# Start bytes of the SBUF tiles: three 32-byte shifts in an encoder layer

## The chip, the cores and the metric

One NeuronCore of a Trainium2 chip runs the kernel: TensorE (PE, whose weight loads the profile lists apart as PEld), VectorE (DVE), ScalarE (ACT), GpSimd (POOL) and SyncE (SP), which issues every DMA here. Data lies in SBUF, a memory of 128 partitions: a tile takes the same byte range in each of them, and "start byte" below is where that range begins, modulo 128. Matmul results lie in PSUM. The metric is the device time of one execution in microseconds, the median of several runs.

## The reference

One layer of an encoder with 1024 channels, run for a prompt of 256 tokens and a sample of 1024 tokens with shared weights (1280 tokens, ten blocks of 128). All data are float32.

```python
def trunk(x, ...):
    x = x + 0.5 * rms_norm(swiglu(rms_norm(x, ffn1_pre_g), ffn1_w_gu, ffn1_w_down), ffn1_post_g)
    x = x + rms_norm(mixer(rms_norm(x, mix_pre_g), w_in, conv_w, ..., w_out), mix_post_g)
    x = x + 0.5 * rms_norm(swiglu(rms_norm(x, ffn2_pre_g), ffn2_w_gu, ffn2_w_down), ffn2_post_g)
    return rms_norm(x, final_g)

def swiglu(h, w_gu, w_down):            # w_gu 1024 x 5632, w_down 2816 x 1024
    gate, up = jnp.split(h @ w_gu, 2, axis=-1)
    return (jax.nn.silu(gate) * up) @ w_down

def mixer(h, ...):
    q, k, v, ga, gb = split(h @ w_in)   # 8 heads of 64, 512 conv channels
    attn = dilated_attention(q, k, v)   # three (window, dilation) branches, merged by softmax weights
    c = silu(layer_norm(depthwise_conv31(ga * sigmoid(gb)) + conv_b))
    return concatenate([attn, c]) @ w_out
```

## The kernel before

Every large product is done three times in float32r: an operand is split into a high part (ACT copies it with rounding) and a low part (DVE subtracts), and `mm3` (lines 196 to 200) issues high x high, high x low (or low x high) and the other mixed product. A TensorE matmul streams the moving operand (`rh` in `mm3`) against a stationary one of 128 x 128 (`lh`) that a weight load brings in just ahead. In the profile's names, as `psd<-wd,ahl`, the first input is the moving one and the second the stationary one.

The order of the work on each engine is that of the code, which interleaves it by hand; the tile framework puts the semaphore waits in. The stages, in order: the first feed-forward block (`ffn`, matmuls into `psgu` with the token tiles `hT` moving and `whi`/`wlo` stationary; into `psd` with `whi`/`wlo` moving and `ah`/`al` stationary), the input projection with the convolution beside it (`w_in`; DVE adds 24 taps per channel group into PSUM, line 744, each reading the tile `glu` from 4 bytes further on), the attention (`attn`; q stationary, `kH` and `kL` moving, lines 952 and 953), `w_out`, and the second feed-forward block: `ffn_gu` first runs two column groups as in the first block, and then `pair`, which forms 7 products out of 8 from token sums (`T2` to `T4`, or `hT` itself) with `wb` as the weights, into `psAB`, `psC` and `psR`; then `ffn_down`, into `psd` with `wd` moving and `ahl` stationary. Ten RMS norms per norm stage go through `rstd` and the stages of `chain`, where `st` is a tile of two numbers per partition.

Where a tile begins follows from the order in which pools are opened. Pools on the left side stack upwards from the start of SBUF: `const` (the 128 x 128 identity `ident`, two scalars, `cv`), `hp` (the `hT` tiles, which later also hold the second block's results, named `yh0h` and so on), `stp` (the small statistics tiles `ast`, `bn`, `st`), `tp` (working tiles `tmp`, `x`, `g`), and then those of the stages: `fy` (`y`), `qk0`, `wc` (`cacc`), `wo1`, `fa2`/`ft2` (`ac`, `T2` to `T4`), `p2` (`wd`, `xr`). Pools with `side="right"` stack downwards from the end: `wp` and later `wp2` (`raw`, `whi`, `wlo`, `wb`, `ahl`, `ar`), `fa` (`ah`, `al`, `sg`), `wg` (`glu`), `att`, `attr` (`pr`, `pT`), `qk1`. Each tile is rounded up to a multiple of 32 bytes. Nearly all big tiles have sizes that are multiples of 128 bytes, so one start byte passes from pool to pool along each side. `run` opens the pools.

Of the kernel before, what the change touches and what calls it, by code (L numbers as in the profile page):

```python
# [10 lines left out]
F32 = mybir.dt.float32  # L11
# [6 lines left out]
P = 128  # L18
# [48 lines left out]
class Stream:  # L67
    def __init__(self, t, units, raw=None, ahead=2):
        self.t, self.units, self.rawp, self.ahead = t, units, raw, ahead
        self.raw, self.w, self.nl, self.nc = {}, {}, 0, 0  # L70
# [78 lines left out]
class Trunk:  # L149
    def __init__(self, tc, ctx, a):  # L150
        self.tc, self.nc, self.ctx, self.a = tc, tc.nc, ctx, a
        nc = self.nc
        self.const = ctx.enter_context(tc.tile_pool(name="const", bufs=1))
        self.ident = self.const.tile([P, P], F32, name="ident")
        make_identity(nc, self.ident)
        self.mhalf = self.const.tile([P, 1], F32, name="mhalf")
        nc.gpsimd.memset(self.mhalf, -0.5)
        self.zero = self.const.tile([P, 1], F32, name="zero")
        nc.gpsimd.memset(self.zero, 0.0)
        self.hp = ctx.enter_context(tc.tile_pool(name="hp", bufs=1))  # L160
        self.stp = ctx.enter_context(tc.tile_pool(name="stp", bufs=4))
        self.tp = ctx.enter_context(tc.tile_pool(name="tp", bufs=2))
        self.psg = ctx.enter_context(tc.tile_pool(name="psg", bufs=4, space=PSUM))
        self.psd = ctx.enter_context(tc.tile_pool(name="psd", bufs=2, space=PSUM))
        self.dp = ctx.enter_context(tc.tile_pool(name="dp", bufs=1, space=DRAM))
        self.hT = {}
        self.stages, self.live, self.ready, self.stale = (), [], [], set()
        self.bg = []
        self.mmn = 0
# [32 lines left out]

    def rstd(self, src, junk, mul):
        nc = self.nc
        st = self.stp.tile([P, 2], F32, name="st", tag="st", bufs=9)
        nc.scalar.activation(junk, src, AF.Square, scale=D ** -0.5 / mul, accum_out=st[:, 0:1])  # L206
        nc.gpsimd.tensor_scalar(st[:, 0:1], st[:, 0:1], 1e-6 / (mul * mul), None, op0=OP.add)  # L207
        nc.gpsimd.tensor_tensor(st[:, 1:2], st[:, 0:1], self.mhalf, op=OP.pow)
        return st[:, 1:2]
# [972 lines left out]
def run(self):  # L1182
# [9 lines left out]
    def pool_(name, **kw):  # L1192
        m = tc.tile_pool(name=name, reuse_waits="tile", **{"bufs": 1, **kw})
        p = m.__enter__()
        return p, lambda: m.__exit__(None, None, None)

    wp, wp_x = pool_("wp", bufs=10, side="right")
    self.wp = wp
    units = self.ffn_units(a["ffn1_w_gu"], a["ffn1_w_down"])
# [139 lines left out]
    self.finish()  # L1339
    p_x()  # L1340
    wp_x()


Trunk.run = run
# [25 lines left out]
```

## Time and profile before

| what | value |
|---|---|
| median of 3 runs | 2439.67 us (2438.82 to 2442.0) |
| profiled execution | 2438.86 us, its span 2437.1 us |
| mean granted TensorE clock | 0.982 |
| busy: PE, PEld, DVE, ACT, POOL | 2350.7, 2009.4, 1263.2, 739.9, 491.5 us |
| moved from and to HBM | 149.23 MB read, 43.73 MB written |

The span is from the first to the last instruction; the profiled execution's own time is 1.8 us longer. Busy time of PE counts the time from a matmul's start to its modelled end, and the matmuls overlap: a 512-wide one is listed with 389 ns, though in a row they start every 0.23 us. So the time that a row of matmuls costs is read from the starts in the timeline, not from the mean length. A row of the grouped views ends with busy time, the mean length of one instruction in ns, and the idle time of the engine before it with what ended it. The view of one line or tile gives lengths as minimum, median and maximum in ns.

### The profile page before, as it was taken

The page shows a single profiled execution, that of the slowest core. Times are in us where ns is not written, and L with a number is a line of the kernel's source. Part 1 is how long each engine was busy: PE and PEld are TensorE (multiplying, and loading weights), DVE is VectorE, ACT ScalarE, POOL GpSimd, SP SyncE. Part 2 cuts the span into 40 slices and gives each one's busy share as a digit, 9 for nine tenths or more (in the row PEclk, how much of TensorE's full clock was granted, in tenths as well). Part 3 has the DMA queues.
Part 4 walks back from the last instruction along what each step waited for, and adds up shares of the span by engine and source line. Part 5 has one row for each costly group of instructions (what it writes and reads, how often), then busy time and mean ns, then how long its engine had stood idle before and what let it go on. Part 6 is the DMA issues. An engine that isn't in the chain of part 4 may idle for free.

```text
span 2437.1 us, 30173 instructions
## 1 busy us (share of the span) xinstructions
PE 2350.7 (96%) x12028; PEld 2009.4 (82%) x12028; DVE 1263.2 (52%) x1695; ACT 739.9 (30%) x1387; POOL 491.5 (20%) x474
## 2 busy tenths in 40 slices
PE   7999999999999998999997799999999999999996
PEld 7888888888888887888886678888888888788885
DVE  5344444444444438899455553564344444454557
ACT  5211111111111125565356552332322222312113
POOL 2000000000000016797202233223232323100004
PEclk9999999999999999999998899999999999999998
DMA  5111111111111115241267552211222222432324
GB/s 179 44 35 44 35 44 35 44 35 44 35 44 35 44 61 164 70 124 61 78 157 148 112 157 95 93 57 61 72 70 68 74 62 84 130 106 68 106 74 154
DMA packets 191827, 194.92 MB, mean 80 GB/s; under 512 B 30212, under 2 KB 154916, under 8 KB 191686
## 3 DMA queue, kind: packets, MB, share of 16 engines
q1 hardware_dynamic: 191686, 193.00, 26.8%
q8 instruction: 94, 1.54, 0.3%
q14 instruction: 47, 0.39, 0.1%
HBM read 149.23 MB, written 43.73 MB: 79 GB/s over the span
## 4 chain that ended last, share of the span: by engine, by line
PE 87%; DMA 5%; DVE 3%; ACT 2%; issue 1%; POOL 1%; SPq 1%; POOLq 0%; ACTq 0%; DVEq 0%
PE psgu L198 9%; PE psgu L199 9%; PE psgu L200 9%; PE psd L198 7%; PE psd L199 7%; PE psd L200 7%; PE psAB L198 4%; PE psAB L199 4%; PE psAB L200 4%; PE psR L199 2%; PE psR L200 2%; PE psR L198 2%; PE psC L198 2%; PE psC L199 2%; PE psC L200 1%; PE psqk L198 1%
## 5 line engine op out<-in xcount | busy, mean ns | idle before, releaser
L390 DVE TENSOR_TENSOR y<-y,psd 128x1024 f32<-128x1024 f32 x190 | 231.6, 1219 | 176.2 <-PE psd L200 176.2
L207 POOL TENSOR_SCALAR st<-st 128x1 f32<-128x1 f32 x70 | 41.7, 596 | 1253.4 <-ACT tmp L206 981.8
L371 DVE TENSOR_TENSOR sg<-sg,psgu 128x512 f32<-128x512 f32 (+1 forms) x66 | 39.5, 599 | 273.0 <-PE psgu L200 273.0
L198 PE MATMUL psd<-wd,ahl 128*128 128x512 f32 x440 | 172.1, 391 | 3.3 <-DVE yh0l L663 1.4
L199 PE MATMUL psd<-wd,ahl 128*128 128x512 f32 x440 | 171.3, 389 | 0.0
L200 PE MATMUL psd<-wd,ahl 128*128 128x512 f32 x440 | 171.2, 389 | 0.0
L198 PE MATMUL psd<-whi,ah 128*128 128x512 f32 x432 | 169.7, 393 | 0.8 <-DVE y L407 0.8
L199 PE MATMUL psd<-wlo,ah 128*128 128x512 f32 x432 | 169.3, 392 | 0.0
L200 PE MATMUL psd<-whi,al 128*128 128x512 f32 x432 | 167.7, 389 | 0.0
L90 ACT ACTIVATE whi<-raw 128x1024 fp32r<-128x1024 f32 x98 | 103.2, 1058 | 212.1 <-PE psgu L199 166.9
L198 PE MATMUL psgu<-hT0h,whi 128*128 128x512 f32 (+1 forms) x416 | 155.9, 375 | 0.0
L198 PE MATMUL psgu<-hT1h,whi 128*128 128x512 f32 (+1 forms) x416 | 155.3, 373 | 0.5 <-ACT hT1h L225 0.5
L199 PE MATMUL psgu<-hT0l,whi 128*128 128x512 f32 (+1 forms) x416 | 155.6, 374 | 0.0
L200 PE MATMUL psgu<-hT0h,wlo 128*128 128x512 f32 (+1 forms) x416 | 155.4, 374 | 0.0
L91 DVE TENSOR_TENSOR wlo<-raw,whi 128x1024 fp32r<-128x1024 f32 x98 | 126.6, 1296 | 55.0 <-ACT whi L90 51.6
L199 PE MATMUL psgu<-hT1l,whi 128*128 128x512 f32 (+1 forms) x416 | 155.0, 373 | 0.0
L200 PE MATMUL psgu<-hT1h,wlo 128*128 128x512 f32 (+1 forms) x416 | 155.0, 373 | 0.0
L115 DVE TENSOR_TENSOR wb<-raw,wb 128x512 fp32r<-128x512 f32 x120 | 84.8, 708 | 106.4 <-ACT wb L114 103.9
L114 ACT ACTIVATE wb<-raw 128x512 fp32r<-128x512 f32 x120 | 75.5, 629 | 167.4 <-PE psC L200 68.0
L744 DVE SCALAR_TENSOR_TENSOR acc<-glu,cv,acc 128x1024 f32<-128x1024 f32 x96 | 121.5, 1284 | 1.8
L372 ACT ACTIVATE ah<-sg 128x512 fp32r<-128x512 f32 (+1 forms) x65 | 35.9, 553 | 253.0 <-DVE sg L371 253.0
L198 PE MATMUL psgu<-hT2h,whi 128*128 128x256 f32 x384 | 109.5, 286 | 2.8 <-DVE hT1l L226 2.8
(356 smaller groups left out, 6124.5 us busy)
## 6 DMA issues: line engine op xcount, KB each, us to landing
raw<-in_ffn_w_gu_dram SPq DMA_DIRECT2D x88, 512.0 KB
raw<-in_ffn_w_down_dram SPq DMA_DIRECT2D x22, 512.0 KB
ad<-ac SPq DMA_DIRECT2D x44, 256.0 KB
g<-in_ffn_w_down_dram SPq DMA_DIRECT2D x22, 512.0 KB
ar<-ad SPq DMA_DIRECT2D x44, 256.0 KB
raw<-in_w_in_dram SPq DMA_DIRECT2D x20, 512.0 KB
x2d<-y SPq DMA_DIRECT2D x10, 512.0 KB
q<-qd SPq DMA_DIRECT2D x16, 320.0 KB
```

The costliest lines, as they stand in the source:

```text
L90: nc.scalar.activation(hi, raw, AF.Copy)
L91: nc.vector.tensor_tensor(lo, raw, hi.bitcast(F32), op=OP.subtract)
L114: nc.scalar.activation(out[:, 0], src, AF.Copy)
L115: nc.vector.tensor_tensor(out[:, 1], src, out[:, 0].bitcast(F32), op=OP.subtract)
L198: mm(out, lh[0], rh[0], start=first, stop=False, skip_group_check=more)
L199: mm(out, lh[0], rh[1], start=False, stop=False, skip_group_check=more)
L200: mm(out, lh[1], rh[0], start=False, stop=last, skip_group_check=more)
L207: nc.gpsimd.tensor_scalar(st[:, 0:1], st[:, 0:1], 1e-6 / (mul * mul), None, op0=OP.add)
L371: nc.vector.tensor_tensor(s[:, :n], s[:, :n], ps[1][:, :n], op=OP.mult)
L372: nc.scalar.activation(ah, s[:, :n], AF.Copy)
L390: nc.vector.tensor_tensor(yb, yb, o, op=OP.add)
L744: nc.vector.scalar_tensor_tensor(V["acc"], gs(k), w(k), V["acc"], op0=OP.mult, op1=OP.add)
```

## The change

Two unused tiles of 8 numbers per partition (32 bytes) are added and the ring of `st` grows from 9 to 10 entries of 32 bytes. Nothing reads or writes the new tiles.

```diff
@@ Trunk.__init__
         nc.gpsimd.memset(self.zero, 0.0)
+        self.pad = self.const.tile([P, 8], F32, name="pad")
         self.hp = ctx.enter_context(tc.tile_pool(name="hp", bufs=1))
@@ rstd
-        st = self.stp.tile([P, 2], F32, name="st", tag="st", bufs=9)
+        st = self.stp.tile([P, 2], F32, name="st", tag="st", bufs=10)
@@ run
+    rp, rp_x = pool_("rp", side="right")
+    rpad = rp.tile([P, 8], F32, name="rpad")
     wp, wp_x = pool_("wp", bufs=10, side="right")
 ...
     wp_x()
+    rp_x()
```

The `pad` shifts everything on the left from `hp` on by 32 bytes, the longer `st` ring what follows `stp` by 32 more, and `rpad` everything on the right by 32 bytes downwards. In the built program the tiles begin here, modulo 128:

| tiles | before | after |
|---|---|---|
| `hT` (and `yh0h`, `yh0l`, `yh2h` in them) | 96 | 0 |
| left side behind the statistics: `tmp`, `x`, `g`, `y`, `cacc`, `T2` to `T4`, `ac`, `wd`, `xr`, the even heads' `q`, `qb`, `kH`, `kL` | 96 | 32 |
| right side: `raw`, `whi`, `wlo`, `wb`, `ah`, `al`, `ahl`, `ar`, `glu`, `sg`, `pr`, `pT`, `v`, the odd heads' `q`, `qb`, `kH`, `kL` | 96 | 64 |
| `ident` | 0 | 0 |
| `ast` (ring of three) | 0, 64, 32 | 64, 0, 96 |

The instructions of each engine, and their order, are the same before and after. Of the waits two differ: of the `rstd` squares on ACT, one in the first norm no longer waits for DVE and one in the last norm no longer for POOL, since the ring of `st` comes round one entry later. The 11,088 float32r matmuls of the built program (7,920 that are 512 wide, 3,168 that are 256 wide) had both operands begin at 96, but for 160 in the attention whose moving operand begins at 32 (the 16 leading elements of `kH` and `kL` are skipped). After the change the moving operand begins at 0 in 6,800 of them, with the stationary one at 64; in 1,980 at 32 against 64 (`T2` to `T4` and `wd`); in 1,420 both begin at 64; the other 888 (mostly `w_out`, the `v` projection and the attention) have other pairs of 0, 32, 64 and 96.

## The prediction

> **What bounds the kernel now.** I read the page first, its busy times and the chain that ended last.
>
> ```profile
> span 2437.1 us, 30173 instructions
> PE 2350.7 (96%) x12028; PEld 2009.4 (82%) x12028; DVE 1263.2 (52%) x1695; ACT 739.9 (30%) x1387; POOL 491.5 (20%) x474
> ...
> PE 87%; DMA 5%; DVE 3%; ACT 2%; issue 1%; POOL 1%; SPq 1%; POOLq 0%; ACTq 0%; DVEq 0%
> ```
>
> TensorE is on the chain for 87% of the span. DMA has 5% (122 us), and DVE, ACT and POOL together 6% (146 us). Next the stages, from the view of stretches (busy us and number of instructions of each engine, granted clock, DMA share, GB/s).
>
> ```profile
> 60.00:940.00 880.00, 875.38 (x4343) 744.65 (x4343) 403.47 (x404) 152.16 (x225) 24.63 (x26) 1.00 0.15 45
> 940.00:1244.00 304.00, 297.93 (x1538) 254.52 (x1539) 231.37 (x225) 152.88 (x271) 183.16 (x200) 0.99 0.30 94
> 1244.00:1440.00 196.00, 161.35 (x949) 142.08 (x949) 113.51 (x454) 125.48 (x384) 43.69 (x26) 0.89 0.69 149
> ...
> 1760.00:2130.00 370.00, 367.00 (x1925) 314.80 (x1924) 155.93 (x224) 107.49 (x180) 97.41 (x67) 1.00 0.26 81
> 2130.00:2437.00 307.00, 287.38 (x1265) 236.80 (x1263) 174.55 (x177) 70.61 (x115) 28.18 (x40) 0.97 0.32 103
> ```
>
> In the feed-forward stages PE is busy for nearly all of the stretch at a granted clock of 1.00; only the attention (1244 to 1440) and the very ends leave it idle. So the question is whether the distance from one matmul to the next changes. The timeline gives it, from the first and last start of two steady rows: 512 columns wide (`wd` moving) and 256 wide (`hT2`).
>
> ```profile
> 2199.89 0.39 PE L198 MATMUL psd<-wd,ahl 128*128 128x512 f32 x1
> ...
> 2213.49 0.39 PE L198 MATMUL psd<-wd,ahl 128*128 128x512 f32 x1
> ```
>
> ```profile
> 300.55 0.28 PE L198 MATMUL psgu<-hT2h,whi 128*128 128x256 f32 x1
> ...
> 302.47 0.28 PE L199 MATMUL psgu<-hT2l,whi 128*128 128x256 f32 x1
> ```
>
> Between the first pair lie 60 steps, 13.60 / 60 = 226.7 ns each; between the second 16, 1.92 / 16 = 120.0 ns. The 256 further columns cost 106.7 ns, so 512 columns are 213.3 ns of streaming and each matmul carries 13.3 ns that don't depend on its width. That is the only sum in this kernel large enough to matter that a start byte might set: over the 11,088 float32r matmuls it is 148 us.
>
> **The added tiles and the longer ring.** `pad` and `rpad` have no instruction, and the list of instructions on each engine is the same, so nothing is added or moved: 0 us. The two waits that fall away are on ACT squares for the tenth block, whose `st` entry was read nine norms earlier; those readers have long run, so 0 us, and what keeps covering them is the wait for the square's own input, which stays.
>
> **TensorE.** The start bytes are what changes, and the term is 11,088 times some change of the 226.7 or 120.0 ns. Its lower bound is all of the 13.3 ns gone, 148 us less. Its upper bound comes from the nearest row in which a matmul starts later than that while the engine is fed: behind 256-wide ones.
>
> ```profile
> 1865.20 0.40 PE L198 MATMUL psC<-hT1h,wb 128*128 128x512 f32 x1
> 1865.43 0.40 PE L199 MATMUL psC<-hT1l,wb 128*128 128x512 f32 x1
> 1865.67 0.39 PE L200 MATMUL psC<-hT1h,wb 128*128 128x512 f32 x1
> ```
>
> 0.24 us after the second one is 13 ns over the steady 226.7, so 148 us more. Between ends so far apart I go by rows that already differ in start byte. The attention has float32r matmuls whose moving operand begins at 32 instead of 96, still with the stationary one at 96, and others (`qb`) whose moving operand isn't one run but eight pieces of 128 bytes, each beginning at 96:
>
> ```profile
> 1293.15 0.28 PE L953 MATMUL pss<-kL,q 128*128 128x256 f32 x1
> 1293.27 0.28 PE L952 MATMUL pss<-kH,q 128*128 128x256 f32 x1
> 1293.39 0.28 PE L953 MATMUL pss<-kL,q 128*128 128x256 f32 x1
> 1293.51 0.38 PE L1060 MATMUL oa<-pT,v 128*128 128x256 f32 x1
> ```
>
> ```profile
> 1305.53 0.28 PE L953 MATMUL pss<-kL,qb 128*128 128x256 f32 x1
> 1305.65 0.28 PE L952 MATMUL pss<-kH,qb 128*128 128x256 f32 x1
> 1305.76 0.28 PE L953 MATMUL pss<-kL,qb 128*128 128x256 f32 x1
> 1305.88 0.59 PE L1060 MATMUL ob<-pT,v 128*128 128x256 f32 x2
> ```
>
> Three steps take 0.36 us at 32 (120 ns each, as at 96) and 0.35 us (117 ns) with eight unaligned pieces. If a read that crosses some 64- or 128-byte line cost part of the 13.3 ns, eight pieces would cost it eight times, and they cost nothing. The stationary side has a row too: the statistics `ast` are loaded as weights from 0, 64 and 32 in turn.
>
> ```profile
> L980 PEld LDWEIGHTS psm<-ident,ast x8: 98/98/153, 1264.9 to 1427.1; 128*36 128x36 f32 x8
> ```
>
> Minimum and median of the eight loads are both 98 ns, and a single one is longer, though the three places take turns. That none of these rows has a float32r operand at 0 or 64 is what stays open. The third question is whether engines that read the same byte range disturb each other, since all stood at 96. Over the 60 steps above they would have had to:
>
> ```profile
> 2199.89:2213.49 13.60, 13.60 (x62) 11.26 (x60) 7.85 (x9) 4.62 (x7) 0.00 (x0) 1.00 0.14 40
> ```
>
> DVE was busy for 7.85 and ACT for 4.62 of these 13.60 us, and every start still came after 0.22 or 0.23 us.  I take 0 of the 148, by the nearness of the attention's rows; both ends stay for the range.
>
> [...]
>
> **DVE, ACT, POOL.** The convolution's taps read `glu` from a place 4 bytes further on each time, so they show every start byte:
>
> ```profile
> L744 DVE SCALAR_TENSOR_TENSOR acc<-glu,cv,acc x96: 1272/1288/1296, 993.3 to 1158.1; 128x1024 f32<-128x1024 f32 x96
> ```
>
> From 1272 to 1296 ns is 1.9%, for 24 different places. If all the 146 us on the chain moved by that, it would be 2.8 us either way; I take 0, as the places 4 bytes apart show no slope.
>
> **DMA.** Every transfer into or out of a big tile begins at another byte. No row shows one transfer from two start bytes; the nearest is the same load by two heads, each its largest piece on the chain:
>
> ```profile
> 1255.28 8.68 DMA kL<-kd
> 1267.97 9.37 DMA kL<-kd
> ```
>
> They differ by 8%, which on 122 us is 10 us either way. I take 0: those two landed at the same start byte (32), so the 8% is something else, and most transfers stay at a byte that is no multiple of 128 (32 or 64 instead of 96). Only the stores of the results, from `yh0h` to `yh2h`, now begin at 0, and nine of ten lie under other work; the last is issued at 2433.52 and has 3.6 us to the span's end.
>
> ```profile
> 2433.52 0.33 SPq L271 DMA_DIRECT2D out_dram<-yh2h  x1
> ```
>
> [...]
>
> **Sum.** Profiled execution 2438.86 (span 2437.1 and 1.8 around it), plus 0 for TensorE, 0 for the vector engines, 0 for DMA. That execution is 0.8 us under the median of the runs, 2439.67; I put the new median between, at 2439.4.
>
> **Rivals.** *The fixed 13.3 ns goes where the moving operand now begins at 0.* For it: that sum is constant over all widths, as a cost of starting a read would be, and no float32r row began at 0. Against it: the eight pieces at 117 ns. It would take 6,800 x 13.3 = 90 us, giving 2349. [...] Chance 5%.
>
> *A smaller gain outside TensorE*, in the transfers of the attention and in the ends of the stages, up to the 10 us of the DMA bound: 2430 to 2434. For it: DMA is 69% busy from 1244 to 1440, where PE waits. Against: only results begin at a rounder byte than 32. Chance 11%.
>
> *Slower: operands at different bytes collide.* Before, moving and stationary operand began at the same byte, and their reads may have run in step; now 1,980 matmuls read 32 against 64 (`T2` to `T4`, `wd`). If one of the two reads were held for 13 ns, that is 1,980 x 13.3 = 26 us, 2466; it decides, at 4.9 us, from 2.5 ns each. Against it: 32 against 96 in the attention costs 120 ns as well. Chance 7%. *Slower by DMA*, the other half of that bound: 2445 to 2450, chance 7%.
>
> *The change doesn't shift the tiles*, or only some: the time would be the same, and the forecast too.
>
> **How the numbers follow.** About 0.2%, 4.9 us, is what a measurement of this kernel can tell from no change; it is 0.44 ns per float32r matmul, so even one nanosecond on each (11.1 us) would be seen. No change has 70%: 2439.4, its own range 2435 to 2444. Faster has 5 + 11 = 16%, slower 7 + 7 = 14%. The range takes in most of the two small rivals, 2430 to 2448; outside are the 12% of the two TensorE cases and a few of the DMA ones.
>
> **What would show it.** Right: in the profile after, the 60 steps of `wd` take 13.60 us and 16 steps of `hT2` take 1.92; PE's busy time is 2351 within 3; the taps lie in 1272 to 1296 ns; the five stretches keep their shares. Wrong by TensorE: a steady distance other than 226.7 or 120.0 ns, in the rows with `hT` moving for the first rival, in `wd` and `T2` to `T4` alone for the slower one. Wrong by DMA: same distances, but the attention's stretch longer or shorter than 196 us.

## The result, and the profile after

The changed kernel takes 2461.01 us (2459.36 to 2461.08), the kernel before 2439.67: a ratio of 1.0083, interval 1.006 to 1.0106. It is slower by 21.3 us. The forecast was 2439.4, in a range of 2430 to 2448.

From the page of the changed kernel, the span, busy times and chain:

```profile
span 2459.2 us, 30173 instructions
PE 2374.7 (97%) x12028; PEld 2004.3 (82%) x12028; DVE 1262.8 (51%) x1695; ACT 740.2 (30%) x1387; POOL 492.4 (20%) x474
...
PE 87%; DMA 4%; DVE 3%; ACT 2%; POOL 2%; issue 1%; SPq 0%; POOLq 0%; ACTq 0%; DVEq 0%
```

DVE, ACT and POOL are busy for the same times within 1 us; PE alone grew, by 24.0 us, and the span by 22.1 (the weight loads, PEld, are busy for 5.1 us less); the mean granted clock was 0.983, before 0.982. Now the steady rows that the prediction measured, from the timeline after: 60 steps of `wd`, and 16 steps of `hT2`.

```profile
2214.69 0.40 PE L199 MATMUL psd<-wd,ahl 128*128 128x512 f32 x1
2214.92 0.39 PE L200 MATMUL psd<-wd,ahl 128*128 128x512 f32 x1
2215.15 0.39 PE L201 MATMUL psd<-wd,ahl 128*128 128x512 f32 x1
2215.39 0.40 PE L199 MATMUL psd<-wd,ahl 128*128 128x512 f32 x1
...
2228.69 0.40 PE L199 MATMUL psd<-wd,ahl 128*128 128x512 f32 x1
```

```profile
302.57 0.28 PE L199 MATMUL psgu<-hT2h,whi 128*128 128x256 f32 x1
...
304.46 0.28 PE L200 MATMUL psgu<-hT2l,whi 128*128 128x256 f32 x1
```

The 60 steps take 14.00 us instead of 13.60, 233.3 ns each instead of 226.7. The 16 steps take 1.89 instead of 1.92, 118 ns instead of 120. The wide matmuls became slower, and the narrow ones faster. A third kind of row, with `hT1` moving and 512 columns, first and last of 48, before and then after:

```profile
80.08 0.39 PE L198 MATMUL psgu<-hT1h,whi 128*128 128x512 f32 x1
...
90.74 0.39 PE L200 MATMUL psgu<-hT1h,wlo 128*128 128x512 f32 x1
```

```profile
80.56 0.40 PE L199 MATMUL psgu<-hT1h,whi 128*128 128x512 f32 x1
...
91.33 0.39 PE L201 MATMUL psgu<-hT1h,wlo 128*128 128x512 f32 x1
```

10.66 / 47 = 226.8 ns before, 10.77 / 47 = 229.1 after. The loss is spread over the whole program, as four places in the timelines show, each the start of the same matmul before and after:

```profile
55.26 0.40 PE L198 MATMUL psgu<-hT2h,whi 128*128 128x256 f32 x2
...
874.00 0.28 PE L198 MATMUL psgu<-hT2h,whi 128*128 128x256 f32 x1
...
1609.17 0.28 PE L198 MATMUL psgu<-hT2h,whi 128*128 128x256 f32 x1
...
2104.69 0.28 PE L199 MATMUL psR<-hT2l,wb 128*128 128x256 f32 x1
```

```profile
55.59 0.40 PE L199 MATMUL psgu<-hT2h,whi 128*128 128x256 f32 x2
...
881.27 0.28 PE L199 MATMUL psgu<-hT2h,whi 128*128 128x256 f32 x1
...
1623.55 0.28 PE L199 MATMUL psgu<-hT2h,whi 128*128 128x256 f32 x1
...
2119.93 0.28 PE L200 MATMUL psR<-hT2l,wb 128*128 128x256 f32 x1
```

Taking differences, the first 55 us lose 0.3 us, the first feed-forward block 6.9, the middle of the layer 7.1, the product pairs 0.9 and the rest, up to the span's end, 6.9: together 22.1. For the kinds of matmul I took, from the single starts in the trace, the mean time from a matmul's start to the next one's, wherever that comes within 300 ns; the last column is its change times their number in the trace of before (`T*` is `T2` to `T4`, "projections" the matmuls of `w_in`):

| rows | before, ns | after, ns | worth, us |
|---|---|---|---|
| `psd<-wd,ahl` | 226.8 | 233.3 | +8.4 |
| `psAB<-T*,wb` | 226.7 | 233.5 | +4.9 |
| `hT` moving, 512 columns (`psgu`, `psC`, `psAB`, projections) | 226.7 to 229.0 | 229.3 to 230.1 | +8.3 |
| `hT` stationary, 512 columns (`pso`, `psv`) | 226.4 to 227.9 | 233.0 to 233.9 | +4.1 |
| `psd<-whi,ah` and its two others | 227.1 to 228.6 | 229.2 to 231.8 | +2.8 |
| `hT2` moving, 256 columns, `psR` | 119.4 | 114.8 | -4.4 |
| `hT2` moving and other 256 columns, `psgu` | 121.5 to 122.3 | 120.1 to 120.8 | -2.2 |
| 256 columns, projections | 119.9 to 121.4 | 117.5 to 128.0 | +0.8 |

With 0.8 for what is left this makes +23.5, of a span longer by 22.1. What remained to be found is what in the start bytes sets this spacing.

### The profile page after: what moved, and what is told of

It is laid out like the page before. It is cut to its first block, busy times and chain, and to the rows that moved or that the text cites. A ratio compares the mean times of both kernels' runs of the same rounds, so it can differ in the third digit from the quotient of the medians.

```text
span 2459.2 us, 30173 instructions
## 1 busy us (share of the span) xinstructions
PE 2374.7 (97%) x12028; PEld 2004.3 (82%) x12028; DVE 1262.8 (51%) x1695; ACT 740.2 (30%) x1387; POOL 492.4 (20%) x474
## 4 chain that ended last, share of the span: by engine, by line
PE 87%; DMA 4%; DVE 3%; ACT 2%; POOL 2%; issue 1%; SPq 0%; POOLq 0%; ACTq 0%; DVEq 0%
PE psgu L199 9%; PE psgu L201 9%; PE psgu L200 9%; PE psd L199 8%; PE psd L201 7%; PE psd L200 7%; PE psAB L200 4%; PE psAB L201 4%; PE psAB L199 4%; PE psqk L199 2%; PE psC L201 2%; PE psC L200 2%; PE psR L201 1%; PE psR L200 1%; PE psR L199 1%; PE psqk L201 1%
## 5 line engine op out<-in xcount | busy, mean ns | idle before, releaser
L199 PE MATMUL psd<-wd,ahl 128*128 128x512 f32 x440 | 175.4, 399 | 2.5 <-DVE yh0l L664 1.4
L200 PE MATMUL psd<-wd,ahl 128*128 128x512 f32 x440 | 173.3, 394 | 0.0
L201 PE MATMUL psd<-wd,ahl 128*128 128x512 f32 x440 | 173.2, 394 | 0.0
L91 DVE TENSOR_TENSOR wlo<-raw,whi 128x1024 fp32r<-128x1024 f32 x98 | 126.2, 1291 | 57.5 <-ACT whi L90 54.0
L745 DVE SCALAR_TENSOR_TENSOR acc<-glu,cv,acc 128x1024 f32<-128x1024 f32 x96 | 121.5, 1284 | 1.8
L371 ACT ACTIVATE sg<-psgu 128x512 f32<-128x512 f32 (+1 forms) x66 | 34.4, 521 | 259.6 <-PE psgu L201 259.6
```

Source lines behind the costliest of these rows:

```text
L91: nc.vector.tensor_tensor(lo, raw, hi.bitcast(F32), op=OP.subtract)
L199: mm(out, lh[0], rh[0], start=first, stop=False, skip_group_check=more)
L200: mm(out, lh[0], rh[1], start=False, stop=False, skip_group_check=more)
L201: mm(out, lh[1], rh[0], start=False, stop=last, skip_group_check=more)
L745: nc.vector.scalar_tensor_tensor(V["acc"], gs(k), w(k), V["acc"], op0=OP.mult, op1=OP.add)
```

## The experiments

Two names for what follows: the spacing is the time from one matmul's start to the next one's in a steady row, and the distance is the start byte of the moving operand minus that of the stationary one, modulo 256 bytes. Counted modulo 256, all the big tiles of the kernel before begin at 224, so nearly every distance there is 0. After the change `hT` begins at 0, the left side at 32 and the right side at 192, so the distance is 64 for the 6,720 matmuls with `hT` moving (the 6,800 ahead of the prediction have 80 of the attention in them), 96 for 1,980 with `wd` or `T2` to `T4`, 192 where `hT` is stationary (32 in half of `pso`, whose weights stand on the left side), and still 0 for the 1,296 of `psd<-whi,ah` and its two others.

**Matmul rows alone, 16 pairs of start bytes.** A kernel that leaves the layer out (its outputs are zeros) and has nothing but rows of 192 matmuls, three per step as in `mm3`, on resident tiles. Moving and stationary operand begin at 0, 32, 64 or 96, named `a` to `d`; first 512 columns (`w`), then 256 (`n`).

```diff
+    for n, w in ((512, "w"), (256, "n")):
+        for m in range(4):
+            for s in range(4):
+                o = rows(nc, ps, M, W, f"{w}mv{LET[m]}st{LET[s]}", 32 * m, 32 * s, n)
```

> A kernel of matmul rows alone: for each of 16 pairs of start bytes (moving 0, 32, 64, 96 by stationary 0, 32, 64, 96, letters a to d in the PSUM tile's name: mv, then st), 192 float32r matmuls in the kernel's pattern of three, 512 wide, and then the same 256 wide. The outputs are zeros. Theory 1 (the pair): the distance between matmuls depends on moving minus stationary byte, so the four equal pairs give 226.7 and 120.0 ns as the kernel did with 96 and 96, and unequal pairs give 229 to 237 ns (512) and 113 to 118 ns (256). Theory 2 (each operand by itself): one row or one column of the table is slow, whatever the other operand, and 0/0, 32/32, 64/64 differ from 96/96. Theory 3 (not the last 7 bits of the address): no pair differs from another by more than 2 ns, and the slow rows of the changed kernel come from something else.

Two of the 32 rows, each by one of its three kinds of matmul (the view of a tile: length as minimum, median, maximum, then the first and last start): both at 64, and 0 against 64.

```profile
L34 PE MATMUL wmvcstc<-mvh,stl x64: 389/389/397, 462.8 to 505.7; 128*128 128x512 f32 x64
```

```profile
L34 PE MATMUL wmvastc<-mvh,stl x64: 393/394/398, 106.6 to 150.7; 128*128 128x512 f32 x64
```

63 steps of three take 42.9 us in the first, 227 ns per matmul, and 44.1 in the second, 233.3. From the single starts (the mean without the first 24 steps): all four equal pairs have 226.7 ns with 512 columns and 120.0 with 256; of the unequal ones the two whose moving operand begins 64 bytes past the stationary one 228.9, the ten others 233.3 to 234.3. With 256 columns every unequal pair took 116.7 to 118.4 but one (120.0). What else worked meanwhile, in the view of stretches:

```profile
100.00:700.00 600.00, 600.00 (x2593) 486.51 (x2592) 9.69 (x14) 0.00 (x0) 0.00 (x0) 1.00 0.00 1
```

Beside 14 copies on DVE (9.69 of 600 us) no other engine was at work, and DMA moved 1 GB/s. TensorE's own two operands suffice. The start byte of one by itself does nothing among these four, since the equal pairs are alike: the theory of the pair holds, and the two others fall.

**Everything at one byte modulo 128.** If equality modulo 128 were the rule, a placement with all tiles at 0 should be as quick as all at 96.

```diff
+        self.pad = self.const.tile([P, 8], F32, name="pad")
 ...
+    rp, rp_x = pool_("rp", side="right")
+    rpad = rp.tile([P, 24], F32, name="rpad")
```

> The kernel before with everything at 0 modulo 128 (hT, left side and right side), by padding alone. Theory 1: operands begin at the same byte again, so the distances are 226.7 and 120.0 ns and the time is 2438 to 2442 us. Theory 2: it depends on what 0 is worth by itself; since the changed kernel has hT at 0 and its 512-wide rows at 229.6 ns, some 2455 to 2465 us. Theory 3: 2440 or 2460, with no link to the bytes.

2473.9 us in a single run, against 2439.27 of the kernel before beside it: the slowest of all, and outside what each theory had given. The rows with `hT` or `wd` moving and 512 columns took 232 to 233 ns. So modulo 128 was the wrong measure: here the left side stands at 0 and the right side at 128 modulo 256.

**Rows alone, twelve distances.** The same kind of kernel, 144 matmuls per row.

```diff
+DIST = {0: "zero", 4: "four", 8: "eight", 16: "sixteen", 32: "x", 64: "xx", 96: "xxx", 128: "xxxx", 160: "xxxxx",
+        192: "xxxxxx", 224: "xxxxxxx", 256: "full"}
 ...
+    for n, w in ((512, "w"), (256, "n")):
+        for d in DIST:
+            o = rows(nc, ps, M, W, f"{w}{DIST[d]}", d, n, 128)
 ...
+    for cols, w in ((64, "half"), (32, "quarter")):
+        for d in (0, 32, 96):
+            o = rows(nc, ps, M, W, f"{w}{DIST[d]}", d, 512, cols)
```

> Matmul rows alone (the outputs are zeros), stationary operand at a fixed place, moving operand 0, 4, 8, 16, 32, 64, 96, 128, 160, 192, 224 and 256 bytes further on (modulo 512; the names zero, four, eight, sixteen, x to xxxxxxx for 32 to 224, full for 256), 144 matmuls each, 512 and then 256 wide; at the end stationary operands of 64 and 32 columns (half, quarter), 512 wide, at 0, 32 and 96. Theory 1b (the distance modulo 256): 0 and 256 give 226.7 and 120.0 ns, 128 gives about 233 (512 wide) as the kernel with all tiles at 0 had; 160, 192 and 224 repeat what -96, -64 and -32 gave: 234, 233 and 233 (512), 117, 118 and 118 (256). If the weight load's read is what the stream collides with, the narrow stationary operands lose less: 32 columns at distance 32 or 96 lie no more than 2 ns over their own distance 0. Theory 2b (the distance modulo 128, and something else made the kernel with all at 0 slow): 128 gives 226.7 and 120.0. Theory 4 (the load has no part in it): 64 and 32 columns lose 6 to 7 ns at 32 and 96 as 128 columns do.

Rows with 128 (`wxxxx`) and 256 bytes (`wfull`), and with 256 columns at 0 (`nzero`) and 192 (`nxxxxxx`):

```profile
L34 PE MATMUL wxxxx<-mvh,sth x48: 392/394/398, 251.4 to 284.3; 128*128 128x512 f32 x48
```

```profile
L34 PE MATMUL wfull<-mvh,sth x48: 389/389/395, 385.9 to 417.9; 128*128 128x512 f32 x48
```

```profile
L34 PE MATMUL nzero<-mvh,sth x48: 278/283/283, 418.6 to 435.5; 128*128 128x256 f32 x48
```

```profile
L34 PE MATMUL nxxxxxx<-mvh,sth x48: 276/276/286, 571.7 to 587.7; 128*128 128x256 f32 x48
```

47 steps take 32.9 us at 128 and 32.0 at 256 (233 and 227 ns), with 256 columns 16.9 at 0 and 16.0 at 192 (120 and 113 ns). So 256 bytes are as good as 0, and 160, 192 and 224 give what -96, -64 and -32 gave in the pairs (234.3, 233.3 and 233.3 ns with 512 columns): the period is 256 bytes. Most distances stand in the table further down. With fewer stationary columns the load is shorter; the 64-column row at distance 0, its weight load and its matmul:

```profile
L34 PEld LDWEIGHTS halfzero<-mvh,sth x48: 134/134/138, 622.3 to 654.6; 128*64 128x64 f32 x48
L34 PE MATMUL halfzero<-mvh,sth x48: 388/394/397, 622.4 to 654.8; 128*64 128x512 f32 x48
```

The load takes 134 ns instead of 188, yet the spacing is 230.0 ns at 0, 230.9 at 32 and 230.0 at 96; with 32 columns it is 231.7, 233.4 and 233.4. The narrow rows lose less to the distance, as expected if the load has a part in it, but at distance 0 they are slower than the full one (226.7), which no theory had said.

**The whole kernel at distance 0, at another byte.** All tiles at 0 modulo 256 instead of 224.

```diff
+        self.pad = self.const.tile([P, 8], F32, name="pad")
 ...
+    rp, rp_x = pool_("rp", side="right")
+    rpad = rp.tile([P, 56], F32, name="rpad")
```

> The kernel before with all big tiles at 0 modulo 256 (before: 224; in the kernel with all at 0 modulo 128 the left side was at 0 and the right side at 128 modulo 256). Theory 1b: all distances are 0 modulo 256 again, 226.7 and 120.0 ns and 2438 to 2442 us. Theory 2b or an effect of the place 0 itself: 2460 to 2475 us.

2436.81 us against 2439.55: the loss of the change is gone, though every start byte is another than in the kernel before. From the kernel with everything at one byte modulo 128 it differs only in `rpad`, which is 128 bytes longer, and these are worth 37 us.

**One part of the change alone.** First the left side at distance 96 (`wd`, `T2` to `T4`, and the half of `pso` with weights there) and `hT` at 0; then `hT` at distance 64 and the left side at 0.

```diff
 left side alone
-        st = self.stp.tile([P, 2], F32, name="st", tag="st", bufs=9)
+        st = self.stp.tile([P, 2], F32, name="st", tag="st", bufs=12)
 hT alone
+        self.pad = self.const.tile([P, 16], F32, name="pad")
-        st = self.stp.tile([P, 2], F32, name="st", tag="st", bufs=9)
+        st = self.stp.tile([P, 2], F32, name="st", tag="st", bufs=15)
```

> One part of the change alone: the left side behind the statistics 96 bytes on, so that T2 to T4 and wd stand 96 past wb and ahl (modulo 256) as in the changed kernel, while hT and the right side stay. Theory 1b: wd and T rows take 233.3 ns in the pattern 231, 232, 237, 2,040 x 6.6 = 13 us, so 2451 to 2455 us; the rows with hT moving stay at 226.7 and 120.0. Rival (the change's cost lies in hT or in other engines): 2438 to 2442 us.

> The other part alone: hT 64 bytes past the right side's tiles (modulo 256) as in the changed kernel, the left side's other tiles equal to the right side's. Theory 1b, by the first table: 3,840 512-wide matmuls x 2.2 = +8 us, 2,880 256-wide ones x -2.2 = -6 us, 720 with hT stationary x 6.7 = +5 us, and some 4 us where rows of equal distance follow unequal ones and need some 8 matmuls to settle: 2448 to 2454 us. Rival (T and wd alone carry the cost): 2438 to 2442 us.

Measured 2455.74 and 2456.14 us, against 2439.55. Sixty steps of `wd` in the timeline, the first kernel and then the second:

```profile
2196.75 0.40 PE L198 MATMUL psd<-wd,ahl 128*128 128x512 f32 x1
...
2210.75 0.40 PE L198 MATMUL psd<-wd,ahl 128*128 128x512 f32 x1
```

```profile
2202.92 0.39 PE L199 MATMUL psd<-wd,ahl 128*128 128x512 f32 x1
...
2216.52 0.39 PE L199 MATMUL psd<-wd,ahl 128*128 128x512 f32 x1
```

14.00 and 13.60 us: the `wd` rows are slow only where the left side was moved. The rows with `hT` behave the other way round: `psgu` with 512 columns at 226.7 ns in the first and 229.5 in the second, and `psv`, which has `hT` stationary, at its old 226 to 227 in the first and 233 to 234 in the second. Both times, of one run each, are above what was expected (2451 to 2455, 2448 to 2454), the first by less than 1 us, while 15 runs of the kernel before spread over 8. The two parts, 16.2 and 16.6 us, sum to 11.4 more than the 21.3 of the change.

By the groups (the kinds of matmul in the table above), the guess for the first left out `pso`, which loses 1.7 us, and rows that kept their distance, which lose some 2. In the second the 256-column rows save 2.3 us and not the 6 expected. Rows at distance 0 lose too when their neighbours are at another one: with `hT` moved, `psd<-whi,ah` and its two others 3.0 us (2.8 in the change) and `T2` to `T4` 1.5.

That the parts don't add up has no single cause. By the groups they lose 9.8 us more than the change: `psR` 2.5 (at the same distance 64 it took 117.8 ns with `hT` alone moved and 114.8 in the change), `T2` to `T4` 2.0, the rows with `hT` stationary 1.8 (half of `pso` loses in both parts), `hT` moving with 512 columns 1.7 and the other 256-column rows of `psgu` 1.7. What a row takes depended a little on the rows beside it, as these 3.0 ns of `psR`.

**Only the distance, not the byte modulo 128.** The kernel before with the right side 128 bytes further down, so every tile stays at 96 modulo 128.

```diff
+    rp, rp_x = pool_("rp", side="right")
+    rpad = rp.tile([P, 32], F32, name="rpad")
```

> The kernel before with only the right side moved by 128 bytes: every tile still begins at 96 modulo 128, but 9,204 matmuls now have their two operands 128 bytes apart modulo 256 (some 6,400 of them of 512 columns). Main theory (the distance modulo 256): 512 columns at 232 to 234 ns and 256 columns at 118 to 119, some 6,400 x 6.5 = 41 us more and 2,800 x 1.3 = 4 us less, 2470 to 2480 us; psd<-whi,ah, whose operands stay at 0, near its 228 ns. Rival (the start byte modulo 128 is what counts): 2437 to 2442 us and no spacing moved.

2472.32 us, against 2440.98 (2437.64 to 2444.97) of the kernel before. The first and last of the 48 `hT1` matmuls that took 10.66 us before:

```profile
80.65 0.40 PE L198 MATMUL psgu<-hT1h,whi 128*128 128x512 f32 x1
...
91.61 0.39 PE L200 MATMUL psgu<-hT1h,wlo 128*128 128x512 f32 x1
```

10.96 us, 233.2 ns each; `psR` went from 119.4 to 118.7, and `psd<-whi,ah` and its others, still at 0, from 228 to 230. One unused tile of 128 bytes costs 31 us, in a single run, and the byte modulo 128 cannot be the cause.

**Rows alone again, in another order.** Distances 0, 16, ... 240.

```diff
+DIST = {16 * i: f"d{chr(97 + i)}" for i in range(16)}
```

> Matmul rows alone (the kernel's computation is left out, outputs are zeros): moving operand 0, 16, 32 ... 240 bytes past the stationary one modulo 256, 512 and 256 columns, 144 matmuls each. Main theory (only the distance modulo 256 sets the spacing): the values that the earlier rows gave come back to 0.1 ns: 512 columns 226.7 at 0, 231.7 at 16, 233.3 at 32, 228.9 at 64, 233.4 at 96; 256 columns 120.0 at 0, 113.3 at 16, 116.6 at 32, 117.8 at 64, 120.0 at 96, 113.3 at 192. For the new distances: 512 columns between 226.7 and 238, none under 226.7; 256 columns between 113.3 and 123. Rival (the row that stood ahead sets the state in which the next row runs): the same distance gives other values here, since other rows stand ahead of it, by more than 1 ns in several of them.

Means from the single starts, ns, of the two runs of rows alone:

| distance | 0 | 16 | 32 | 64 | 96 | 128 | 160 | 192 | 224 | 256 |
|---|---|---|---|---|---|---|---|---|---|---|
| 512 columns, first order | 226.7 | 231.7 | 233.3 | 228.9 | 233.4 | 233.4 | 234.3 | 233.3 | 233.3 | 226.7 |
| 512, second order | 226.7 | 231.7 | 233.4 | 228.9 | 233.3 | 232.4 | 234.3 | 233.4 | 233.3 | |
| 256 columns, first order | 120.0 | 113.3 | 116.6 | 117.8 | 120.0 | 118.7 | 117.4 | 113.3 | 118.3 | 120.0 |
| 256, second order | 120.0 | 118.7 | 116.7 | 117.8 | 120.0 | 118.7 | 117.3 | 113.3 | 118.3 | |

With 512 columns the distance fixes the spacing, to 0.1 ns but for 128. No distance was under 226.7; the worst was 4, at 237.9. The other steps of 16 gave 231 to 235, and 240 gave 226.7 again. With 256 columns most come back too, but 16 gave 113.3 once and 118.7 once: there the rival, that the row ahead chooses between states, has a point. The pairs of the first experiment had 117.8 at 192, where both orders here gave 113.3.

**A version to beat both.** Since 0 is the best for 512 columns and among the worst for 256, `hT2`, whose rows as moving operand all have 256 columns, gets a distance of its own: 192 on top of the placement at 0 modulo 256, with the tiles behind it padded back to 0.

```diff
+        if t == 2:
+            self.hp.tile([P, 48], F32, name="hpad", tag="hpad")
         self.hT[t] = ...
-        st = self.stp.tile([P, 2], F32, name="st", tag="st", bufs=9)
+        st = self.stp.tile([P, 2], F32, name="st", tag="st", bufs=11)
```

> The kernel with every pair of operands at distance 0 modulo 256 except hT2, which begins 192 bytes past the right side's weights, where the rows alone took 113.3 ns instead of 120.0 with 256 columns. Main theory: 2,496 matmuls with hT2 as moving operand, up to 6.7 ns each, 16.6 us, less 0.6 us for the 144 of 512 columns that read hT2 as stationary operand, and less what the first matmuls of each row take to settle: 2421 to 2428 us, psR spacing 113 to 115 ns, wd steps unchanged at 226.7. Rival 1 (the short rows never settle in the kernel): 2433 to 2438 us. Rival 2 (TensorE is no longer the only bound once it is faster, so waits take the gain): the spacing falls, but the time stays within 3 us of 2436.8.

> All operands at 0 modulo 256, so the distances between them modulo 256 are those of the kernel before, which has all at 224. Main theory: the spacings are the same and so is the time, 2436 to 2440 us, ratio 0.998 to 1.000; what is left of the 2.7 us in the single look comes from no matmul row. Rival (the start byte itself counts a little, beside the distance): 2434 to 2437.5 us with an interval wholly below 1, and spacings of 512 columns lower by 0.5 to 1 ns.

Against 2441.04 us of the kernel before (2436.65 to 2444.62 in 15 runs): 2430.56 with `hT2` at 192, ratio 0.996 (0.9947 to 0.9972); 2437.44 without, ratio 0.9987 (0.9978 to 0.9996). The first is faster than the kernels before and after the change. The first and last of the 16 `hT2` steps:

```profile
299.29 0.28 PE L201 MATMUL psgu<-hT2h,whi 128*128 128x256 f32 x1
...
301.17 0.28 PE L202 MATMUL psgu<-hT2l,whi 128*128 128x256 f32 x1
```

1.88 us, 117.5 ns, and 117.8 in `psR`, not the 113.3 of the rows alone: it is the spacing that the pairs of the first experiment had at 192, the other of the two states. So the time is 2430.6, between the 2421 to 2428 expected and the rival's 2433 to 2438. From the groups, the 256-column rows give back 4.8 us and the 512-column ones beside them 1.6 (`hT` moving 1.2, `psd<-whi,ah` and its others 0.6, `pso` and `psv` lose 0.2); the profiled span is 7.3 us shorter than before. For the placement at 0 alone the interval lies just below 1, as both theories allow, but no row is faster: each group of float32r matmuls is worth the same within 0.2 us. What makes those 3.6 us, if they are real, stays open, and they are a third of the 10.5 above.

**`hT2` 32 bytes off.** The kernel before with `hT2` alone at distance 32, where both orders had agreed on 116.7.

```diff
+        if t == 2:
+            self.hp.tile([P, 8], F32, name="hpad", tag="hpad")
-        st = self.stp.tile([P, 2], F32, name="st", tag="st", bufs=9)
+        st = self.stp.tile([P, 2], F32, name="st", tag="st", bufs=16)
```

> The kernel before with hT2 alone 32 bytes past the right side's weights, all else at distance 0. The rows alone gave 116.7 ns at 32 in both orders in which they were run, against 120.0 at 0, and 113.3 at 192, where the kernel had 117.5. Main theory as it now stands (a distance other than 0 has several states and the rows ahead choose between them): spacing of the 256-column rows 115 to 119 ns, 2,496 x 1 to 5 ns, 2428 to 2437 us. Rival (the distance alone sets it): 116.7 ns to 0.3, and 2430 to 2433 us.

2438.44 us, ratio 0.9986 (0.9976 to 0.9996), `psR` at 116.9 and long `psgu` rows at 116.7: the spacing that the distance alone gives, but less time saved than either theory said (2428 to 2437, 2430 to 2433). The 256-column groups save 3.6 us; the 512-column ones give 1.2 back, 0.7 of it in `pso` and `psv`, which read `hT2` as stationary operand, now at 224. The comparison of times has 2.5.

## Why the prediction was wrong

**The failed step is "I take 0 of the 148, by the nearness of the attention's rows".** It put the cost of unequal start bytes for 512-column rows at nothing, from rows of 256 columns. Those rows did differ in distance (64 and 192 by the count modulo 256), but with 256 columns these distances cost nothing: 117.8 ns at 64 and 113 to 118 at 192 against 120.0 at 0, in the rows alone. With 512 columns the same distances cost 2.2 and 6.6 ns, and 96 costs 6.6, which no row of before could show, since there all 512-column rows stood at 0.

The two attention rows were also read too finely. "120 ns each" and "117 ns" are 0.36 and 0.35 us over three steps, from starts rounded to 0.01 us. By the single starts in the trace of before both take 353 ns, 117.7 each. So the row "as at 96" was already 2.3 ns faster than a row at distance 0, and "32 against 96 in the attention costs 120 ns as well" was not so: a sign that the distance mattered lay under the rounding. (The eight pieces of a `qb` row begin at distances 0 and 128 in turn.) The 98 ns of the `ast` loads compare lengths of loads, and the length of a load did not move with the change in the 512-column rows (187 or 188 ns in the median of each kind, before and after); what moved is the spacing of the matmuls.

**The 13.3 ns.** They were taken as one cost that doesn't depend on width, since 256 further columns cost 106.7 ns. At distance 192 they cost 120.0 (233.3 less 113.3), so what a distance adds is not a fixed sum per matmul. The first bound, all of it gone, was never near at 512 columns: 226.7 is the least of all rows; with 256 the distance took half of them at best (113.3 for 120.0, in the rows alone). The upper bound of 13 ns more was twice the 6.6 that came; it too was read from rounded starts, which are 235 ns apart in the trace, 8 ns over.

**The rivals.** "Operands at different bytes collide" was right that a pair at unequal bytes costs time, and had 7%; that it is a collision stays open. It named 1,980 matmuls at 13.3 ns, 26 us. They cost 6.7 ns each, 13.3 us by the groups; 9.4 us more came from rows that it left out (`hT` moving and stationary, and their neighbours, +15.2) and from the 256-column ones that gained (-5.8). So its 2466 was near by luck, two errors that cancel. Its condition, 2.5 ns each, was met. The argument against it, 120 ns in the attention, is the failed step again. "The fixed 13.3 ns goes where the moving operand begins at 0" fell: with 512 columns those rows are slower, by 2.3 ns in the steady row shown, and of those with 256 `psR` is faster by 4.6, far from 13.3. The rivals outside TensorE fell, as the next point shows. That the tiles don't shift fell with the rows.

**Other engines, DMA, added tiles.** These zeros held. The taps took 1267 to 1291 ns, where 1272 to 1296 was forecast, and the attention's `pss` matmuls lie between the same two starts as before, 166.5 us and then 165.9, in the view of the tile before and after:

```profile
L953 PE MATMUL pss<-kL,q x80: 277/282/420, 1244.9 to 1411.4; 128*128 128x256 f32 x80
```

```profile
L954 PE MATMUL pss<-kL,q x80: 275/282/420, 1256.5 to 1422.4; 128*128 128x256 f32 x80
```

The DMA bound of 10 us was not needed. That engines reading beside TensorE don't disturb it holds too: the rows alone show the spacings of the kernel's steady rows (226.7 ns at 0, 233.3 at 96).

**The forecast's own test** worked: "a steady distance other than 226.7 or 120.0 ns ... in `wd` and `T2` to `T4` alone for the slower one" is what the trace shows, except for "alone".

**What stays open.** The cause of the loss, the distance, is shown; how it acts is not. That the next weight load and the running matmul collide is supposed; no run shows it. For it speak that the distance of the two operands decides, with a period of 256 bytes, that it was worth up to 11 ns of 227 in the rows alone (237.9 ns at 4 bytes), where hardly anything else was at work (in the first of these runs DVE for 9.69 of 600 us), and that in the row shown from that run, both operands at 64, each load starts at most 0.01 us behind a matmul's start and lasts 187 or 188 ns of the 227. Against it speaks that shorter loads don't help: with 64 and 32 stationary columns the rows take 230.0 and 231.7 ns at distance 0, more than with 128. A row without weight loads was not tried. Nor is it known what chooses the state of a 256-column row.

## What to carry to other kernels

Where TensorE bounds a float32r kernel, as here (87% of the chain), print the start bytes of both matmul operands modulo 256 and their difference: unused tiles of 32 to 224 bytes ahead of the pools moved this one between 2430 and 2474 us. Keep the difference at 0 for 512-column rows (226.7 ns here, and no other gave less), try others for 256-column ones (113.3 to 123.4 ns, with 120.0 at 0), and read the spacing from the starts over many steps of a steady row: three steps rounded to 0.01 us can't show 2 ns each. And a price of zero taken from rows of one width is not yet one for another: the change here cost 6.5 ns a matmul with 512 columns (`wd`, 226.8 to 233.3) and saved 4.6 with 256 (`psR`, 119.4 to 114.8).

## What the runs showed that I had not expected

- The spacing of 512-column float32r matmuls depends on the distance of their operands modulo 256 bytes: 226.7 ns at 0 and 240, 228.9 at 64, 231 to 238 elsewhere; 4 bytes are enough for 237.9 (each distance in one or two rows).
- With 256 columns distance 0 is among the slow ones: 120.0 ns, against 113.3 at 112 and 192, and up to 123.4 at 4.
- Such rows can have two steady spacings at the same distance: 113.3 and 118.7 ns at 16, 113.3 and 117.8 at 192, 114.8 and 117.8 at 64 (`psR` after the change, and with `hT` alone moved).
- At distance 0 a row behind unequal ones needs some matmuls to come back to its pace: in `psd<-whi,ah` and its two others after the change the first spacing of a row is 231.4 ns on the mean, and 226.7 comes with the eleventh (before 229.3, and 226.8 with the sixth). So rows with unchanged operands lost 2.8 us beside the changed ones.
